# Gate matrix laid out by chunk of experts and read in three pieces; odd rows of v in u's buffers

## The chip, the cores and the metric

One core of a Trainium2 chip runs the whole program. The metric is the device time of one execution in microseconds (us); less is better.

## The reference

One layer of a streaming encoder over 512 tokens of width 1024: token mixing (sparse attention and pooling), then channel mixing by PEER: each token picks, in 8 heads, its best 16 of 128 x 128 = 16384 experts, each expert being one row of u and one of v. The part that matters here, cut down:

```python
def peer_ffn(h, w_q, sub_keys, u, v):
    ...
    expert = (i1 * N_KEYS + i2).reshape(TOKEN_BLOCK, PEER_HEADS * PEER_TOPK)
    gate = jax.nn.softmax(best_s, axis=-1).reshape(...)
    u_sel = u[expert]
    v_sel = v[expert]
    act = jax.nn.gelu(jnp.einsum('nd,ned->ne', hx, u_sel), approximate=False)
    return jnp.einsum('ne,ned->nd', gate * act, v_sel)
```

## The kernel before

For three of the four blocks of 128 tokens (384 tokens, `ND`) the kernel does not gather: it computes the activation of all 16384 experts for all tokens and multiplies it by a dense matrix of gates that is zero where a token did not pick an expert. The fourth block gathers its 128 rows of u and of v per token (the sparse branch, `sparse`, gathers issued by POOL, sums on DVE). The experts come in 128 groups of 128 (`NEXP`); c is the number of a group throughout.

Stages, in order of time (us from the start of the span):

- to about 480: token mixing, norms, the keys of PEER, the first dense activations.
- about 480 to 740, the gates stage: `gates` builds the dense gates, 16 tokens at a time, into a tile `st` of [128, 128 groups, 16 tokens], 8 KB a partition, and line 629 writes it to the DRAM tile `gd`: 24 writes of 1 MB. Beside it run the dense activations (`dense_acts`): the transposed u of a group is loaded (`ue`, 512 KB, line 527, two buffers in pool `up`), split by ACT into a high part (`uhe`, 517) and by DVE into the rest (`ule`, 518), and multiplied (`pse`, 554 to 556). 59 groups are done here; 22 of their results (`ad`) go to DRAM.
- about 740 to 1598, the contraction: for each c the gates of the group multiply its activations (`gated`, line 727), the product is split (`Wh`, 737, and `Wl`, 739), the row block v of the group (512 KB, line 735) is loaded and split by ACT (`vh`, 738) and DVE (`vl`, 740), and 18 matmuls (line 748, `contract`) add into six accumulators. For c from 0 to 21 the loop only reads an earlier activation back (`gelu..b`, 778); for c from 22 to 90 it also computes one of the remaining activations (538 to 540); from c = 91 on (the tail) it is contraction alone, beside the last of the sparse branch.

The gates come back from `gd` in 16 reads, one for 8 groups (`GJ`), line 725: 24 runs of 512 bytes a partition, 1.5 MB. Their tile `g` has two buffers in pool `vp`, and so has `v`.

The order on DVE, PE and ACT in the contraction is written out by hand (the `manual_schedule` block at the end). SP issues all plain loads and stores, in one queue, in an order that a scheduler derives; an issue that waits (for its buffer to be read out, say) holds everything behind it on SP. A load of v(c+2) waits until `vl(c)` has read its buffer; with two buffers, at most two v are on their way or in use.

```python
            gts[0] = vp.tile([P, ND // GT, GJ, GT], F32, tag="g", name=f"g{c}")
            nc.sync.dma_start(out=gts[0], in_=gd[:, :, c:c + GJ, :].rearrange("g p e t -> p g e t"))
```

Of the kernel before, what the change touches and what calls it, by code (L numbers as in the profile page):

```python
# [9 lines left out]
F32 = mybir.dt.float32  # L10
# [6 lines left out]
ALU = mybir.AluOpType  # L17
# [3 lines left out]
P = 128  # L21
S = 512
D = 1024
DT = D // P
# [9 lines left out]
DENSE = 3  # L34
ND = DENSE * P
NEXP = 128
GT = 16
GJ = 8
# [7 lines left out]
RATE = 3.0  # L46
REST = 7
UPS = 2
SCALED = 14
STB = 2  # L50
FILLS = [(2, 1), (2, 5), (3, 0), (3, 1), (3, 2), (3, 3), (3, 4), (3, 5), (3, 6), (3, 7)]
# [14 lines left out]
def layer(ctx, tc, xT, cvec, w_ada, cols, consts, w_in, w_grp, w_up, w_out, w_pq, subk, u, uT, v, out):  # L66
    nc = tc.nc
    V, A, T, G = nc.vector, nc.scalar, nc.tensor, nc.gpsimd
# [10 lines left out]
    g2row = tc.dram_tile([1, D], F32, name="g2row")  # L79
    x2d = tc.dram_tile([TB, P, D], F32, name="x2d")  # L80
    ad = tc.dram_tile([SPILL, P, ND], F32, name="ad")
    gd = tc.dram_tile([ND // GT, P, NEXP, GT], F32, name="gd")
    nc.sync.dma_start(out=col, in_=cols)
    eps = keep.tile([P, 1], F32, name="eps")
    V.memset(eps, EPS)
# [4 lines left out]
    with ExitStack() as pre:  # L90
# [83 lines left out]
        blocks += [(f"ga{j}", w_in[B_GA + j], DT) for j in range(2)]  # L174
        blocks += [(f"up{j}", w_up[1, j], 4) for j in range(UPS)]
        blocks += [(f"ga{j}", w_in[B_GA + j], DT) for j in range(2, DT)]
        blocks += [(f"up{j}", w_up[1, j], 4) for j in range(UPS, DT)]
        blocks += [(f"ua{j}", w_up[0, j], 4) for j in range(DT)]
# [22 lines left out]
        with ExitStack() as mix:  # L201
# [207 lines left out]
            def up_pool(j):  # L409
                V.tensor_tensor(yp[:, j, :], yp[:, j, :], linear(f"up{j}", pTh, pTl, 4), op=ALU.mult)  # L410

            for j in range(DT):
                tc.keep_in_program_order(A.activation(yp[:, j, :], yp[:, j, :], AF.Sigmoid))
                if j < UPS:
                    up_pool(j)
# [46 lines left out]

            fills = [partial(gate, j) for j in range(2, DT)] + [partial(up_pool, j) for j in range(UPS, DT)]
            for tb in range(TB):
# [47 lines left out]
    up = ctx.enter_context(tc.tile_pool(name="up", bufs=2, side="right", reuse_waits="tile"))  # L512
# [18 lines left out]
    def multiply(w, n, name):  # L531
        return multiplies([w], n, [name])[0]
# [11 lines left out]
    KEPT = HOLD - 1  # L544
# [23 lines left out]
    with ExitStack() as win:  # L568
# [23 lines left out]
        def gates(tb):  # L592

            tr = ptr.tile([P, 4, P], F32, tag="tr", name=f"gtr{tb}")
            for i, x in enumerate(sel[tb]):
                T.transpose(tr[:, i, :], x, ident)

            keys = oh.tile([P, 2, P], F16, tag="keys", name=f"keys{tb}", bufs=1)
            part = oh.tile([P, 2, P], F16, tag="part", name=f"part{tb}", bufs=1)
            gs = oh.tile([P, P], F32, tag="gs", name=f"gs{tb}", bufs=1)  # L600
            A.copy(keys, tr[:, 0:2, :])
            A.activation(gs, tr[:, 2, :], AF.Copy, scale=2.0 ** SCALED)
            A.copy(part[:, 0, :], gs)
            V.tensor_tensor(part[:, 1, :], gs, part[:, 0, :], op=ALU.subtract)

            full = [P, 4, NEXP, 2]
            pairs = lambda x, t: x[:, t:t + 8].rearrange("p (q j) -> p q j", j=2).unsqueeze(2).to_broadcast(full)
            numbers = irep.unsqueeze(1).to_broadcast(full)
            for g in range(P // GT):
                st = oh.tile([P, NEXP, GT], F32, tag="st", name=f"st{tb}_{g}", bufs=STB)  # L610
                for t8 in range(0, GT, 8):
                    t = g * GT + t8
                    one, two = [oh.tile(full, F16, tag=f"on{i}", name=f"on{i}_{tb}_{t}") for i in range(2)]
                    V.tensor_tensor(one, numbers, pairs(keys[:, 0, :], t), op=ALU.is_equal)  # L614
                    V.tensor_tensor(two, numbers, pairs(keys[:, 1, :], t), op=ALU.is_equal)  # L615
                    gated = []
                    for i in range(2):
                        x = oh.tile(full, F16, tag=f"oa{i}", name=f"oa{i}_{tb}_{t}")
                        gated.append(x)
                        V.tensor_tensor(x, one, pairs(part[:, i, :], t), op=ALU.mult)  # L620
                    for t4 in range(0, 8, 4):
                        ps = pgm.tile([P, 4, P], F32, tag="gm", name=f"gm{tb}_{t + t4}")
                        for k in range(4):
                            q, j = (t4 + k) // 2, k % 2
                            for i in range(2):
                                T.matmul(ps[:, k, :], two[:, q, :, j], gated[i][:, q, :, j], start=(i == 0), stop=(i == 1))  # L626
                        A.activation(st[:, :, t8 + t4:t8 + t4 + 4].rearrange("p e t -> p t e"), ps, AF.Copy, scale=2.0 ** -SCALED)  # L627
                        yield
                nc.sync.dma_start(out=gd[tb * (P // GT) + g], in_=st)

        sel = {}

# [45 lines left out]
    vp = ctx.enter_context(tc.tile_pool(name="vp", bufs=2, reuse_waits="tile"))  # L678
# [33 lines left out]
    def residual(tb):  # L712
        x = gp.tile([P, D], F32, tag="row", name=f"xr{tb}")
        nc.sync.dma_start(out=x, in_=x2d[tb])
        return x

    rows = sparse()
    gts = {}
    wei = {}

    def gated(c):

        if c % GJ == 0:
            gts[0] = vp.tile([P, ND // GT, GJ, GT], F32, tag="g", name=f"g{c}")
            nc.sync.dma_start(out=gts[0], in_=gd[:, :, c:c + GJ, :].rearrange("g p e t -> p g e t"))
        wv = gelus[c].rearrange("p (g t) -> p g t", t=GT)
        V.tensor_tensor(wv, wv, gts[0][:, :, c % GJ, :], op=ALU.mult)

    def weights(c):

        last = c == NEXP - 1
        vr = vp.tile([P, D], F32, tag="v", name=f"v{c}")
        vh, vl = [(gp if last else vp).tile([P, D], F32R, tag="row" if last else t, name=f"{t}{c}") for t in ("vh", "vl")]
        wh, wl = [(hold if last else vp).tile([P, ND], F32R, tag="gelu" if last else t, name=f"{t}{c}") for t in ("Wh", "Wl")]
        nc.sync.dma_start(out=vr, in_=v[c * P:(c + 1) * P, :])
        w = gelus.pop(c)
        A.activation(wh, w, AF.Copy)  # L737
        A.activation(vh, vr, AF.Copy)  # L738
        V.tensor_tensor(wl, w, wh.bitcast(F32), op=ALU.subtract)
        V.tensor_tensor(vl, vr, vh.bitcast(F32), op=ALU.subtract)  # L740
        wei[c] = (vh, vl, wh, wl)
# [11 lines left out]
    def ahead(c):  # L753
        if c < NEXP:
            pending[c] = fetch(uT[c], f"e{c}", tc.keep_in_program_order)

    with tc.manual_schedule(engines={mybir.EngineType.DVE, mybir.EngineType.PE, mybir.EngineType.Activation}):
        gated(0)
        weights(0)
        gated(1)  # L760
        V.tensor_copy(ei3, e3)
        due = -DELAY
        late = (2 * P + DELAY - EARLY * SPILL - RATE * (NEXP - KEPT - SPILL)) / (KEPT - REST)
        for c in range(NEXP):
            a = c + KEPT
            if c + 1 < NEXP:
                weights(c + 1)
            if c + 2 < NEXP:
                gated(c + 2)
            if c >= SPILL - 1:  # L770
                ahead(a + 1)
            due += EARLY if c < SPILL else RATE if c < NEXP - KEPT else late
            while due >= 1:
                next(rows, None)
                due -= 1
            if c < SPILL:
                gelus[a] = hold.tile([P, ND], F32, tag="gelu", name=f"gelu{a}b")
                nc.sync.dma_start(out=gelus[a], in_=ad[c])
            elif a < NEXP:
                gelus[a] = hold.tile([P, ND], F32, tag="gelu", name=f"gelu{a}")  # L780
                A.activation(gelus[a], multiply(pending.pop(a), ND, f"e{a}"), AF.Gelu)
            if c == NEXP - REST + 1:
                for _ in rows:
                    pass
                x = residual(DENSE)
                for i in range(2):
                    finish(DENSE, x, i, sacc[:, i * 512:(i + 1) * 512])
            if c < NEXP - 2:
                for tb in range(DENSE):
                    contract(c, tb)  # L790

        xs = [residual(tb) for tb in range(DENSE)]
        for tb in range(DENSE):
            for halves in (((0,), (1,)) if tb == DENSE - 1 else ((0, 1),)):
                for c in (NEXP - 2, NEXP - 1):
                    contract(c, tb, halves)
                for i in halves:
                    finish(tb, xs[tb], i, acc[tb][i])
# [172 lines left out]
```

## Time and profile before

| what | value |
|---|---|
| time, three runs | 1596.89, 1600.07, 1604.06 us (median 1600.07) |
| profiled execution: its time | 1600.14 us |
| profiled execution: its span, first to last instruction | 1598.3 us |
| PE busy | 1540.0 us, 96% of the span |
| DVE busy | 1311.6 us, 82% |
| ACT busy | 691.3 us, 43% |
| POOL busy | 326.1 us, 20% |
| DMA | 393.91 MB, mean 246 GB/s |
| mean granted TensorE clock | 0.991 |
| share of the chain that ended last: PE, DVE, DMA | 48%, 10%, 5% |

The profile lists how long each engine was busy, the chain of work that ended last (followed back from the last instruction to what released each step), the groups of instructions with their durations, and what each engine waited for. PE is the matrix engine, ACT and DVE work on vectors, POOL issues the gathers, SP (SPq) issues the other transfers. The 5% of DMA in the chain is loads of v.

### The profile page before, as it was taken

What the parts mean: (1) busy time and instruction counts of PE and PEld (TensorE: products, weight loads), DVE (VectorE), ACT (ScalarE), POOL (GpSimd) and SP (SyncE); (2) the same over time, 40 slices, a digit from 0 to 9 for tenths busy, and PEclk for the clock granted to TensorE, in tenths of its full rate; (3) what the DMA queues carried; (4) which work ended last, traced back from release to release, by engine and by line L of the source; (5) the groups of instructions that cost most, each with busy time, mean ns of one, the idle gap of its engine ahead of it and who ended that gap; (6) DMA issues with size and microseconds to landing.
All of it is one profiled execution on the core that took longest, in us unless ns stands there. A gap on an engine that the chain in (4) does not pass through costs nothing.

```text
span 1598.3 us, 22373 instructions
## 1 busy us (share of the span) xinstructions
PE 1540.0 (96%) x7977; PEld 1311.7 (82%) x7977; DVE 1311.6 (82%) x2658; ACT 691.3 (43%) x993; POOL 326.1 (20%) x318
## 2 busy tenths in 40 slices
PE   5999999999999999999999999999999999999998
PEld 3678766786789888899778999999999999987776
DVE  7799776658999999995668888888888888887777
ACT  4543445534446675674333333333333333333332
POOL 0000000000000000001113444444544445442320
PEclk9999999999999999999999999999999999999999
DMA  8412654333235454669889999999999999987874
GB/s 309 165 66 86 214 186 121 117 148 119 66 119 195 163 190 173 229 234 322 301 288 340 322 364 332 339 360 316 361 336 337 355 318 363 339 289 261 273 274 171
DMA packets 155105, 393.91 MB, mean 246 GB/s; under 512 B 13041, under 2 KB 67953, under 8 KB 151922
## 3 DMA queue, kind: packets, MB, share of 16 engines
q1 hardware_dynamic: 118130, 258.25, 46.5%
q0 software_dynamic: 36864, 134.23, 23.8%
q8 instruction: 62, 1.02, 0.3%
q14 instruction: 49, 0.40, 0.1%
HBM read 358.75 MB, written 33.69 MB: 246 GB/s over the span
## 4 chain that ended last, share of the span: by engine, by line
PE 48%; DVE 10%; DMA 5%; ACT 1%; issue 1%; SPq 0%; ACTq 0%; DVEq 0%
PE acc L748 28%; PE pse L540 6%; PE pse L539 6%; PE pse L538 6%; DMA v<-v 5%; DVE oa L620 2%; DVE ule L518 2%; DVE on L614 1%; DVE on L615 1%; ACT vh L738 1%; DVE vl L740 1%; PE pse L556 1%; PE pse L555 1%; PE pse L554 1%; PE gm L626 0%
## 5 line engine op out<-in xcount | busy, mean ns | idle before, releaser
L689 POOL DMA_INDIRECT ur<-u,ei x128 | 158.0, 1234 | 638.7 <-ACT Wh L737 395.0
L748 PE MATMUL acc<-vh,Wh 128*128 128x512 f32 x768 | 240.3, 394 | 14.6 <-ACT vh L738 14.6
L748 PE MATMUL acc<-vl,Wh 128*128 128x512 f32 x768 | 241.2, 395 | 2.0 <-DVE vl L740 1.9
L748 PE MATMUL acc<-vh,Wl 128*128 128x512 f32 x768 | 240.1, 394 | 0.0
L740 DVE TENSOR_TENSOR vl<-v,vh 128x1024 fp32r<-128x1024 f32 x128 | 156.9, 1226 | 83.0 <-ACT vh L738 70.7
L697 POOL DMA_INDIRECT vr<-v,ei x128 | 165.2, 1291 | 232.7 <-DVE sacc L702 204.2
L540 PE MATMUL pse<-h2h,ule 128*128 128x384 f32 x552 | 185.1, 335 | 0.0
L539 PE MATMUL pse<-h2l,uhe 128*128 128x384 f32 x552 | 184.6, 334 | 0.0
L538 PE MATMUL pse<-h2h,uhe 128*128 128x384 f32 x552 | 184.4, 334 | 0.0
L737 ACT ACTIVATE Wh<-gelu 128x384 fp32r<-128x384 f32 x106 | 55.6, 525 | 290.1 <-PE acc L748 187.5
L748 PEld LDWEIGHTS acc<-vh,Wh 128*128 128x128 f32 x768 | 144.7, 190 | 41.6 <-ACT vh L738 16.7
L748 PEld LDWEIGHTS acc<-vl,Wh 128*128 128x128 f32 x768 | 145.7, 191 | 35.3 <-DVE vl L740 5.3
L748 PEld LDWEIGHTS acc<-vh,Wl 128*128 128x128 f32 x768 | 146.2, 190 | 30.9
L518 DVE TENSOR_TENSOR ule<-ue,uhe 128x1024 fp32r<-128x1024 f32 x128 | 155.9, 1218 | 19.0 <-ACT uhe L517 19.0
L554 PE MATMUL pse<-h2h,uhe 128*128 128x384 f32 x472 | 166.2, 352 | 1.0 <-ACT gelu L563 1.0
L556 PE MATMUL pse<-h2h,ule 128*128 128x384 f32 x472 | 161.1, 342 | 4.7 <-DVE ule L518 4.5
L702 DVE SCALAR_TENSOR_TENSOR sacc<-vr,wt,sacc 128x1024 f32<-128x1024 f32 x127 | 162.8, 1282 | 2.4
L555 PE MATMUL pse<-h2l,uhe 128*128 128x384 f32 x472 | 159.6, 338 | 0.0
L517 ACT ACTIVATE uhe<-ue 128x1024 fp32r<-128x1024 f32 x128 | 134.8, 1053 | 53.8 <-PE pse L555 36.0
L691 DVE SCALAR_TENSOR_TENSOR ur<-ur,hx 128x1024 f32<-128x1024 f32 x128 | 150.7, 1220 | 1.5 <-DMA ur<-u,ei 1.5
L738 ACT ACTIVATE vh<-v 128x1024 fp32r<-128x1024 f32 x128 | 135.7, 1060 | 36.0 <-DMA v<-v 35.7
L627 ACT ACTIVATE st<-gm 128x512 f32<-128x512 f32 x96 | 101.2, 1092 | 53.9 <-PE gm L626 49.6
(412 smaller groups left out, 2757.3 us busy)
## 6 DMA issues: line engine op xcount, KB each, us to landing
ue<-uT SPq DMA_DIRECT2D x128, 512.0 KB
v<-v SPq DMA_DIRECT2D x128, 512.0 KB
wada<-w_ada SPq DMA_DIRECT2D x48, 512.0 KB
gd<-st SPq DMA_DIRECT2D x24, 1024.0 KB
g<-gd SPq DMA_DIRECT2D x16, 1536.0 KB
ad<-gelu SPq DMA_DIRECT2D x22, 192.0 KB
wgp<-w_in SPq DMA_DIRECT2D x8, 512.0 KB
wga<-w_in SPq DMA_DIRECT2D x8, 512.0 KB
```

What stands on the lines that cost most here:

```text
L518: V.tensor_tensor(lo, src, hi.bitcast(F32), op=ALU.subtract)
L538: T.matmul(p, hi[:, k, :], h2h[:, k, :n], start=(k == 0), stop=False)
L539: T.matmul(p, hi[:, k, :], h2l[:, k, :n], start=False, stop=False)
L540: T.matmul(p, lo[:, k, :], h2h[:, k, :n], start=False, stop=(k == DT - 1))
L554: T.matmul(ps, hi[:, k, :], h2h[:, k, :ND], start=(k == 0), stop=False)
L555: T.matmul(ps, hi[:, k, :], h2l[:, k, :ND], start=False, stop=False)
L556: T.matmul(ps, lo[:, k, :], h2h[:, k, :ND], start=False, stop=(k == DT - 1))
L689: G.indirect_dma_start(out=ur, out_offset=None, in_=u, in_offset=bass.IndirectOffsetOnAxis(ap=ei3[:, k:k + 1], axis=0))
L697: G.indirect_dma_start(out=vr, out_offset=None, in_=v, in_offset=bass.IndirectOffsetOnAxis(ap=ei3[:, k:k + 1], axis=0))
L702: V.scalar_tensor_tensor(sacc, vr, wt[:, k:k + 1], sacc, op0=ALU.mult, op1=ALU.add)
L740: V.tensor_tensor(vl, vr, vh.bitcast(F32), op=ALU.subtract)
L748: T.matmul(acc[tb][i], x[:, t], y[:, i * 512:(i + 1) * 512], start=(c == 0 and n == 0), stop=(c == NEXP - 1 and n == 2))
```

## The change

1. `gd` gets another shape: [16 chunks of 8 groups, 128 partitions, 24 blocks of 16 tokens, 8, 16]. The whole of a chunk is now 12 KB in one run for a partition. A write of `st` (line 629) becomes 16 runs of 512 bytes a partition instead of one of 8 KB.
2. The read of a chunk's gates becomes three reads (`gate_piece`), each 4 KB in one run a partition, 512 KB. They are asked for in the groups 1, 3 and 5 of the chunk before; chunk 0's before the contraction starts. The tile, its size and its two buffers stay.
3. From c = 93 on, odd c load v into the two `u` buffers of pool `up`, which the last u has left; even c keep the two buffers of `vp`. So the tail has four buffers for v.

```diff
-    gd = tc.dram_tile([ND // GT, P, NEXP, GT], F32, name="gd")
+    gd = tc.dram_tile([NEXP // GJ, P, ND // GT, GJ, GT], F32, name="gd")
...
-                nc.sync.dma_start(out=gd[tb * (P // GT) + g], in_=st)
+                nc.sync.dma_start(out=gd[:, :, tb * (P // GT) + g].rearrange("c p e t -> p c (e t)"),
+                                  in_=st.rearrange("p (c e) t -> p c (e t)", e=GJ))
...
+    GP = P // GT
+
+    def gate_piece(n, i):
+
+        if i == 0:
+            gts[n] = vp.tile([P, ND // GT, GJ, GT], F32, tag="g", name=f"g{n}")
+        nc.sync.dma_start(out=gts[n][:, i * GP:(i + 1) * GP], in_=gd[n, :, i * GP:(i + 1) * GP])
 
     def gated(c):
 
-        if c % GJ == 0:
-            gts[0] = vp.tile([P, ND // GT, GJ, GT], F32, tag="g", name=f"g{c}")
-            nc.sync.dma_start(out=gts[0], in_=gd[:, :, c:c + GJ, :].rearrange("g p e t -> p g e t"))
+        n, e = c // GJ, c % GJ
+        if e in (1, 3, 5) and n + 1 < NEXP // GJ:
+            gate_piece(n + 1, e // 2)
         wv = gelus[c].rearrange("p (g t) -> p g t", t=GT)
-        V.tensor_tensor(wv, wv, gts[0][:, :, c % GJ, :], op=ALU.mult)
+        V.tensor_tensor(wv, wv, gts[n][:, :, e, :], op=ALU.mult)
...
-        vr = vp.tile([P, D], F32, tag="v", name=f"v{c}")
+        if c >= NEXP - KEPT + UGAP and c % 2:
+            vr = up.tile([P, DT, P], F32, tag="u", name=f"v{c}").rearrange("p k e -> p (k e)")
+        else:
+            vr = vp.tile([P, D], F32, tag="v", name=f"v{c}")
...
+        for i in range(DENSE):
+            gate_piece(0, i)
         gated(0)
```

The instructions of PE and DVE, and their order, stay as they were (two splits of u change places on ACT). What moves is SP's queue. In the tail, around the gates of groups 104 to 111 (`g104` before, `g13`, the chunk's number, after), SP has before:

```order
L735 DMA v94_13412<-v 128x1024
L735 DMA v95_13444<-v 128x1024
L735 DMA v96_13481<-v 128x1024
L725 DMA g104_13715<-gd_71 128x24x128
L735 DMA v97_13513<-v 128x1024
L735 DMA v98_13545<-v 128x1024
L735 DMA v99_13577<-v 128x1024
```

and after the change:

```order
L747 DMA v95_13472<-v 128x1024
L747 DMA v94_13440<-v 128x1024
L747 DMA v96_13507<-v 128x1024
L747 DMA v97_13541<-v 128x1024
L747 DMA v98_13573<-v 128x1024
L728 DMA g13_13517<-gd_71 128x1024 x2
L747 DMA v99_13606<-v 128x1024
L728 DMA g13_13517<-gd_71 128x1024
L747 DMA v100_13638<-v 128x1024
```

Two pieces stand together behind v98, the third behind v99; v95, which now has another buffer, stands ahead of v94. In the first part of the contraction, around the gates of groups 16 to 23, SP has before:

```order
L778 DMA gelu44b_7940<-ad_70 128x384
L735 DMA v8_7926<-v 128x1024
L725 DMA g16_8171<-gd_71 128x24x128
L735 DMA v9_7960<-v 128x1024
L778 DMA gelu45b_7974<-ad_70 128x384
```

and after:

```order
L792 DMA gelu44b_7946<-ad_70 128x384
L747 DMA v8_7930<-v 128x1024
L728 DMA g2_7940<-gd_71 128x1024
L792 DMA gelu45b_7980<-ad_70 128x384
L728 DMA g2_7940<-gd_71 128x1024
L747 DMA v9_7966<-v 128x1024
L792 DMA gelu46b_8015<-ad_70 128x384
L728 DMA g2_7940<-gd_71 128x1024
L747 DMA v10_8000<-v 128x1024
```

Here v9 stands behind two pieces and one read of an activation, v10 behind the third piece.

## Rows read from the trace of the kernel before

**Rows 1.** Page part 5, costliest groups: the two splits of v
```profile
L740 DVE TENSOR_TENSOR vl<-v,vh 128x1024 fp32r<-128x1024 f32 x128 | 156.9, 1226 | 83.0 <-ACT vh L738 70.7
L738 ACT ACTIVATE vh<-v 128x1024 fp32r<-128x1024 f32 x128 | 135.7, 1060 | 36.0 <-DMA v<-v 35.7
```

**Rows 2.** Chain in order of time, contraction: start us, us, what
```profile
772.64 5.54 DMA v<-v
...
780.62 10.44 DMA v<-v
...
816.21 11.28 DMA v<-v
...
1410.72 4.09 PE acc L748 x18
...
1437.73 12.29 DMA v<-v
...
1477.46 11.53 DMA v<-v
...
1515.75 11.76 DMA v<-v
...
1529.98 56.94 PE acc L748 x243
```

**Rows 3.** Timeline of SP: start us, us, engine, line, operation, count
```profile
776.72 0.37 SPq L725 DMA_DIRECT2D g<-gd  x1
780.62 3.04 SPq L735 DMA_DIRECT2D v<-v  x1
...
1434.12 0.38 SPq L725 DMA_DIRECT2D g<-gd  x1
```

**Rows 4.** Timeline of ACT, line 737, first and last of each stretch read
```profile
785.69 0.53 ACT L737 ACTIVATE Wh<-gelu 128x384 fp32r<-128x384 f32 x1 [2.28 <-PE acc L748]
...
801.16 0.53 ACT L737 ACTIVATE Wh<-gelu 128x384 fp32r<-128x384 f32 x1 [2.31 <-PE acc L748]
...
821.56 0.53 ACT L737 ACTIVATE Wh<-gelu 128x384 fp32r<-128x384 f32 x1 [1.89 <-PE acc L748]
...
836.38 0.53 ACT L737 ACTIVATE Wh<-gelu 128x384 fp32r<-128x384 f32 x1 [4.42 <-PE acc L748]
...
1439.01 0.53 ACT L737 ACTIVATE Wh<-gelu 128x384 fp32r<-128x384 f32 x1 [2.56 <-PE acc L748]
...
1458.32 0.53 ACT L737 ACTIVATE Wh<-gelu 128x384 fp32r<-128x384 f32 x1 [3.83 <-PE acc L748]
...
1478.74 0.53 ACT L737 ACTIVATE Wh<-gelu 128x384 fp32r<-128x384 f32 x1 [2.56 <-PE acc L748]
...
1496.63 0.53 ACT L737 ACTIVATE Wh<-gelu 128x384 fp32r<-128x384 f32 x1 [3.16 <-PE acc L748]
...
1517.03 0.53 ACT L737 ACTIVATE Wh<-gelu 128x384 fp32r<-128x384 f32 x1 [2.56 <-PE acc L748]
...
1551.32 0.53 ACT L737 ACTIVATE Wh<-gelu 128x384 fp32r<-128x384 f32 x1 [2.32 <-PE acc L748]
```

**Rows 5.** Windows: stretch, length, PE, PEld, DVE, ACT, POOL busy (count), PEclk, DMA share, GB/s
```profile
560.00:600.00 40.00, 38.33 (x297) 34.86 (x296) 40.00 (x119) 28.97 (x35) 0.00 (x0) 1.00 0.54 193
...
920.00:1400.00 480.00, 480.00 (x2443) 438.87 (x2442) 405.69 (x497) 173.91 (x235) 224.49 (x174) 1.00 0.97 343
...
1445.00:1450.00 5.00, 2.54 (x12) 1.76 (x10) 0.00 (x0) 0.00 (x0) 0.24 (x1) 1.00 1.01 403
```

**Rows 6.** DMA queue view, 812.6 to 819 us: packets, MB, share of 16 engines
```profile
q1 hardware_dynamic: 1520, 1.30, 72.4%
```

**Rows 7.** The same view, 1555 to 1565 us
```profile
q1 hardware_dynamic: 451, 1.62, 50.8%
```

**Rows 8.** Timeline of SP, gates stage
```profile
494.68 0.33 SPq L629 DMA_DIRECT2D gd<-st  x1
495.10 4.94 SPq L527 DMA_DIRECT2D ue<-uT  x2
```

**Rows 9.** DMA view, 494.5 to 504 us: busy tenths in 40 slices
```profile
DMA  0000996999599796956999940092799982000000
```

**Rows 10.** Timeline of ACT, gates stage: the split of that u
```profile
503.48 1.06 ACT L517 ACTIVATE uhe<-ue 128x1024 fp32r<-128x1024 f32 x1
```

More of the change, by code (lines that the diff above doesn't have):

```diff
@@ L48 @@
 UPS = 2
+UGAP = 2
 SCALED = 14
```

## The prediction

> **What bounds the kernel now.** I read the chain first, then the timelines of SP and ACT, then the DMA views. In the contraction PE sets the pace: the 18 matmuls of a group take 4.09 us, and from 920 to 1400 us PE is busy for all of the 480 us [rows 2, 5]. The chain leaves PE where it goes through a load of v. Five of those loads take 10.44 to 12.29 us, against 5.54 us for one with no gates ahead of it [rows 2]. SP shows why: the read of a chunk's gates is issued at 776.72 and at 1434.12, and the next v, at 780.62 and 1437.73, is the one that takes 10.44 and 12.29 us [rows 2, 3]. The first of these also holds SP for 3.04 us where other issues take some 0.3 [rows 3].
>
> How late may a v be? It is issued when its buffer is free, that is when the rest split of v two groups earlier ends; it must land, be split by ACT (1.06) and by DVE (1.23) within two groups. 2 x 4.09 - 1.06 - 1.23 - 0.1 for gaps = 5.8 us [rows 1, 2]. A clean load (5.54) just fits; one behind the gates is 4.6 to 6.5 us late.
>
> What that costs PE I read from ACT's split of the weights, which follows PE group by group [rows 4]. From 785.69 to 801.16 lie 3 groups: 15.47 - 3 x 4.09 = 3.20 us lost. From 821.56 to 836.38 lie 2: 6.64. In the tail, 3 groups from 1439.01: 7.04; 3 from 1478.74: 5.62; 7 from 1517.03: 5.66. The start of the contraction loses 9.84 us, the tail 18.32, together **28.16 us**. Between groups 22 and 90, where a group takes twice as long because u is multiplied too, nothing is lost.
>
> **The change part by part.** The sum is made against the profiled execution's 1600.14 us (1.84 us more than its span), which is the median of the runs, 1600.07, to within 0.1.
>
> *Reads of 4 KB.* The reads are 16 x 1.5 MB before and 48 x 512 KB after, the same bytes. In a stretch with much of the gates' read, SP's queue kept 72.4% of 16 engines busy for 6.4 us with 1520 packets and 1.30 MB; taken as packets of 4 KB and 512 bytes, that is about 146 and 1374 [rows 6]. In a stretch with v alone 1.62 MB, or 396 packets of 4 KB, took 50.8% of 16 x 10 us, 0.205 us each [rows 7]. So the first stretch spent 74.1 - 146 x 0.205 = 44.1 us on 1374 small packets, 0.032 us each: 4 KB in small pieces cost 0.257 us against 0.205. The reads get 20% cheaper for the engines. This alone takes 20% of the 6.75 us (12.29 - 5.54) by which the worst v was delayed, 1.4 us.
> The Trainium skill (DMA: Bandwidth & Descriptors, Specifications) gives 512 bytes as the transfer size from which the line rate is reached. By it this part would bring nothing, each piece below would delay v 25% longer (1.8 us where I take 1.4, 2.25 where I take 1.8), and the sum would end some 2.5 us higher, at 1580; the rows put 512 bytes 25% above 4 KB, so I take the rows.
>
> *Three pieces, start of the contraction.* v9 and v10 now stand behind pieces of a third (the second pair of orders above). A whole read delayed v by 10.44 - 5.54 = 4.9 and 11.28 - 5.54 = 5.7 us [rows 2], mean 5.3; a third at 80% is 1.4. So v9 takes about 6.9 us, 1.2 more than the 5.8 that are free. I count that as PE's loss once in each of the two chunks, 2.4 us. From below it is 0, if the rest split may be that much later than the first matmul; from above twice that, 4.8, since v8 and v10 share a buffer and two delays may add. The value is taken in the middle, as it is nearest to the single delay of the rows. **Gain 9.84 - 2.4 = 7.4 us.**
>
> *Tail: pieces and four buffers.* The queue goes in pairs, v98 with v99, v100 with v101. An even v still has 5.8 us. An odd v has been free for long but stands behind its even neighbour on SP, so it gets one group more, 9.9 us. v99 has two pieces and v98 ahead: 5.54 + 6.75 x 2/3 x 0.8 + 1.3 (v98's 0.52 MB at the 403 GB/s of 1445 to 1450 [rows 5]) = 10.4, late by 0.5. v100 has one piece ahead: 5.54 + 1.8 = 7.3, late by 1.5. One delay of 1 us per chunk is my value, 3 us for three chunks; the ends are 0 and 2.1 x 3 = 6.3. **Gain 18.32 - 3 = 15.3 us.**
>
> *The writes.* The same 24 MB, in 2048 packets of 512 bytes where there were 128 of 8 KB. No row shows such a write. As a bound from the read's price, 2048 / 16 x 0.032 = 4.1 us a write. Today a write is issued at 494.68 with a u right behind it at 495.10; by slice 24 (500.2 us) both are in, so 1.57 MB took some 4.8 us and the write 3.2 of it [rows 8, 9]. The u is used at 503.48 [rows 10]: 3.3 us to spare, 2.4 with the slower write. I take 0. It cannot be a gain, as no step waits for a write there; if the cover went, DVE would pay in full, since it is busy for 40.00 of 40 us in that stage [rows 5].
>
> *Edits at nothing.* Groups 22 to 90: twice the matmul time per group covers the loads, and PE has no idle time to give back [rows 5]. The gates were already asked for a chunk ahead, so reading ahead is not new. The last two v move ahead of two stores of the result: from 1529.98 on the chain is PE alone for 56.94 us [rows 2], so nothing follows. 32 more issues on SP at about 0.3 us lie in a queue that mostly waits for buffers.
>
> Sum: 1600.14 - 7.4 - 15.3 = 1577.4; I forecast **1577 us**. Its own bounds are 1600.14 - 28.16 = 1572 with no loss left, and 1572 + 4.8 + 6.3 = 1583 with both upper ends.
>
> **The rivals.**
> *A, half stays.* The pieces are not spread: two stand together and the third follows one v later, so within two groups the queue still carries 1.5 MB of gates. If SP's order, not the number of buffers, decides, each stop shrinks to half: 1600.14 - 14.1 = 1586 us. For it speaks the order itself; against it that v98 has passed before the first piece. Chance 0.2.
>
> *B, the bytes decide.* In the tail 8 groups need 4.2 MB of v, 1.6 of gates and at least 4.2 of gathered rows in 32.7 us, some 305 GB/s; pieces don't change that. If the engines are as good as full, the stops only move to another v, and what is left is the 20% of cheaper packets: 0.2 x 28 = 5.6 us, 1594 us, no measurable change. Against it: 343 GB/s over 480 us and 403 over 5 [rows 5].
> The Trainium skill (DMA: Bandwidth & Descriptors, Bandwidth) has the rule that transfers should be batched to 1 MiB or more to reach 75% of the peak, which speaks for B, as pieces of 512 KB would use the engines worse than one of 1.5 MB. Most of the traffic from 920 to 1400 us is loads of 512 KB, and the share is 0.97 at 343 GB/s, so the trace does not bear it out where transfers overlap. Chance 0.09.
>
> *C, the writes come late: slower.* If a small packet costs twice as much written as read, 0.064 us, a write takes 8.2 us, 5.0 more than today, and the u behind it comes 5.0 - 3.3 = 1.7 us late. DVE has no room there, so 24 times that is 41 us: 1577 + 41 = 1618 us. It begins to cost at (3.2 + 3.3) x 16 / 2048 = 0.051 us a packet. For it: the DVE row, and that not every u has so much to spare. Against it: DMA's share there is only 0.54 [rows 5], and most u are not right behind a write. Chance 0.06.
>
> **How the numbers follow.** The forecast gets what remains, 0.65. A difference under 0.5%, 8 us, can't be told from none; the bounds are 1592 and 1608. The forecast's case lies under 1592 wholly, of A's 0.2 about 0.17; B is "same" with the rest of A; C is slower. So faster 0.82, same 0.12, slower 0.06. The range 1570 to 1590 holds the forecast's case and most of A.
>
> **What would show it.** Right: on ACT's line 737 no gap far over 4.09 us from 1420 on, and one or two of about 1 us between 785 and 840; no load of v over 8 us in the chain unless it is an odd one in the tail; the gates stage as long as before, with the first matmul of the contraction at the same time. Wrong: a chain that still has v loads of 10 us (A or B, told apart by whether they stand behind pieces), or waits for u and DVE idle time between 480 and 740 us (C).

## The result, and the profile after

Four runs of the changed kernel took 1574.20 to 1575.62 us, median **1574.58**; four of the kernel before, beside them, had a median of 1598.94. The ratio is **0.9844**, 95% interval [0.9819, 0.9869]: faster by 1.3 to 1.8%. The forecast was 1577, range 1570 to 1590. The profiled execution took 1574.86 us with a span of 1573.1, against 1600.14 and 1598.3; the sums below are of spans.

The page of the changed kernel: part 4 (shares of the chain), then part 5, the splits of v (they answer to [rows 1]), then part 6, issues with their count, size and median us to landing.

```profile
PE 51%; DVE 10%; DMA 2%; ACT 1%; issue 0%; SPq 0%; ACTq 0%; DVEq 0%
...
L752 DVE TENSOR_TENSOR vl<-v,vh 128x1024 fp32r<-128x1024 f32 x128 | 156.8, 1225 | 59.0 <-ACT vh L750 58.8
...
L750 ACT ACTIVATE vh<-v 128x1024 fp32r<-128x1024 f32 x128 | 135.9, 1062 | 9.8 <-DMA v<-v 9.4
...
v<-v SPq DMA_DIRECT2D x128, 512.0 KB, 5.8
...
gd<-st SPq DMA_DIRECT2D x24, 1024.0 KB, 5.9
g<-gd SPq DMA_DIRECT2D x48, 512.0 KB, 8.0
```

DMA's share of the chain fell from 5% to 2%, and the time for which ACT stood waiting for v from 35.7 us to 9.4. The splits themselves cost what they did.

Its chain in order of time (start us, us, what), to be read against [rows 2]:

```profile
735.10 7.17 DMA g<-gd
...
777.22 5.92 DMA v<-v
...
785.58 8.14 DMA v<-v
...
814.81 8.29 DMA v<-v
...
1412.20 149.47 PE acc L760 x659
```

No load of v is left in the tail: from 1412 us PE runs 659 matmuls with no gap, where the kernel before left PE three times. At the start two loads of 8.1 and 8.3 us stand where 10.44 and 11.28 stood. The first row is new: a read of gates is now in the chain.

How much PE lost is read from ACT's split of the weights, as in [rows 4], but over whole stretches, so that one yardstick serves every kernel here: from group 2 to 22 (the start), and from 91 to 127 (the tail). The shortest stretches seen in any run are 81.65 and 150.26 us; what a kernel has above them is its loss. From group 22 to 91 every run takes 565.7 to 566.1. The four splits of the kernel before (start us, us, ..., idle before them):

```profile
757.08 0.53 ACT L737 ACTIVATE Wh<-gelu 128x384 fp32r<-128x384 f32 x1 [2.22 <-PE acc L748]
...
848.67 0.53 ACT L737 ACTIVATE Wh<-gelu 128x384 fp32r<-128x384 f32 x1 [2.56 <-PE acc L748]
...
1414.43 0.52 ACT L737 ACTIVATE Wh<-gelu 128x384 fp32r<-128x384 f32 x1 [3.19 <-DVE sacc L702]
...
1583.15 0.52 ACT L737 ACTIVATE Wh<-gelu 128x384 fp32r<-128x384 f32 x1 [1.76 <-DVE gelu L727]
```

and of the changed kernel, with two splits of v between them:

```profile
758.05 0.53 ACT L749 ACTIVATE Wh<-gelu 128x384 fp32r<-128x384 f32 x1 [3.09 <-PE acc L760]
...
788.58 1.06 ACT L750 ACTIVATE vh<-v 128x1024 fp32r<-128x1024 f32 x1 [1.40 <-DMA v<-v]
...
793.82 1.06 ACT L750 ACTIVATE vh<-v 128x1024 fp32r<-128x1024 f32 x1 [1.82 <-DMA v<-v]
...
841.89 0.53 ACT L749 ACTIVATE Wh<-gelu 128x384 fp32r<-128x384 f32 x1 [1.84 <-PE acc L760]
...
1407.65 0.52 ACT L749 ACTIVATE Wh<-gelu 128x384 fp32r<-128x384 f32 x1 [3.19 <-DVE sacc L704]
...
1557.91 0.53 ACT L749 ACTIVATE Wh<-gelu 128x384 fp32r<-128x384 f32 x1 [1.76 <-DVE gelu L736]
```

Start: 848.67 - 757.08 = 91.59, a loss of 9.94; now 83.84, a loss of 2.19. Tail: 168.72, a loss of 18.46; now 150.26, none. That is 26.2 us gained. The contraction begins 0.97 us later (758.05 against 757.08), and 26.2 - 1.0 = 25.2 is the difference of the spans, 1598.3 - 1573.1. So all of it is accounted for.

Windows of the changed kernel (columns as in [rows 5]):

```profile
480.00:720.00 240.00, 231.87 (x1777) 211.17 (x1776) 237.19 (x687) 161.54 (x200) 0.00 (x0) 1.00 0.64 198
920.00:1400.00 480.00, 480.00 (x2443) 438.79 (x2442) 405.37 (x494) 172.62 (x235) 221.07 (x174) 1.00 0.94 343
```

and the first of them before:

```profile
480.00:720.00 240.00, 231.76 (x1780) 210.95 (x1779) 237.19 (x688) 161.53 (x200) 0.00 (x0) 1.00 0.56 198
```

The writes in runs of 512 bytes show as DMA share: 0.64 against 0.56 at the same 198 GB/s. Over 240 us and 24 writes that is 0.08 x 240 / 24 = 0.8 us of all 16 engines per write. DVE is busy for the same 237.19 us: it costs nothing there. From 920 to 1400 the share fell from 0.97 to 0.94 for the same bytes.

### The profile page after: what moved, and what is told of

Same layout as the page of the kernel before. It is cut to its first block, busy times and chain, and to the rows that moved or that the text cites. A ratio compares the mean times of both kernels' runs of the same rounds, so it can differ in the third digit from the quotient of the medians.

```text
span 1573.1 us, 22413 instructions
## 1 busy us (share of the span) xinstructions
PE 1530.7 (97%) x7977; PEld 1307.4 (83%) x7977; DVE 1311.7 (83%) x2658; ACT 690.2 (44%) x993; POOL 324.9 (21%) x318
## 4 chain that ended last, share of the span: by engine, by line
PE 51%; DVE 10%; DMA 2%; ACT 1%; issue 0%; SPq 0%; ACTq 0%; DVEq 0%
PE acc L760 30%; PE pse L541 6%; PE pse L540 6%; PE pse L539 6%; DVE ule L519 2%; DVE oa L621 2%; DMA v<-v 1%; DVE on L615 1%; DVE on L616 1%; PE pse L557 1%; PE pse L556 1%; PE pse L555 1%; DMA g<-gd 0%; PE gm L627 0%; ACT vh L750 0%
## 5 line engine op out<-in xcount | busy, mean ns | idle before, releaser
L760 PE MATMUL acc<-vl,Wh 128*128 128x512 f32 x768 | 237.1, 390 | 1.0 <-DVE vl L752 1.0
L760 PE MATMUL acc<-vh,Wh 128*128 128x512 f32 x768 | 236.8, 389 | 0.0
L760 PEld LDWEIGHTS acc<-vl,Wh 128*128 128x128 f32 x768 | 143.9, 188 | 31.9 <-DVE vl L752 2.1
```

The source lines that it names most:

```text
L760: T.matmul(acc[tb][i], x[:, t], y[:, i * 512:(i + 1) * 512], start=(c == 0 and n == 0), stop=(c == NEXP - 1 and n == 2))
```

## Experiments

The change has three parts: the layout, the pieces, the tail's buffers. Kernels e1 to e4 and e7 switch these parts on and off, e5 and e6 ask what makes the gates' read slow, and e8 to e10 lend v the buffers at the start too. In the contraction the order of the instructions on PE and DVE is the same in all of them. Medians are in us, ratios are to the kernel before, run beside each; the losses are those of one profiled execution each, read as above, so where they vary from one execution to the next the median can lie apart from them.

| kernel | median | ratio, 95% | start | tail |
|---|---|---|---|---|
| before | 1598.94 to 1603.04 | | 9.94 | 18.46 |
| changed | 1574.58 | 0.9844 [0.9819, 0.9869] | 2.19 | 0 |
| pieces alone (e1) | 1587.85 | 0.9919 [0.9892, 0.9946] | 6.72 | 10.02 |
| layout alone (e2) | 1578.18 | 0.9868 [0.9842, 0.9894] | 0.93 | 3.59 |
| layout, pieces (e3) | 1576.77 | 0.9861 [0.9830, 0.9892] | 1.01 | 1.22 |
| tail's buffers alone (e4) | 1580.51 | 0.9880 [0.9855, 0.9906] | 8.58 | 0 |
| one read, runs of 4 KB (e5) | 1580.21 | 0.9855 [0.9823, 0.9887] | 4.25 | 6.57 |
| before, no gathers of v (e6) | 1581.58 | 0.9868 [0.9839, 0.9897] | 11.86 | 0 |
| layout, tail's buffers (e7) | 1575.34 | 0.9825 [0.9795, 0.9854] | 5.88 | 0 |
| layout, buffers at both ends (e8) | 1571.55 | 0.9807 [0.9783, 0.9831] | 0 | 0 |
| buffers at both ends alone (e9) | 1571.46 | 0.9805 [0.9778, 0.9832] | 0 | 0 |
| changed, buffers at both ends (e10) | 1572.03 | 0.9810 [0.9783, 0.9838] | 0 | 0 |
| changed, again (e11) | 1575.13 | 0.9832 [0.9804, 0.9860] | 4.97 | 0 |
| changed, writes twice (e12) | 1614.19 | 1.0081 [1.0052, 1.0109] | 5.51 | 0 |

(A fourth run of e5 took 2942.69 us, at a granted clock of 0.932 where its others have 0.996 and 0.997; it is not in the median.)

**e1, the pieces alone**, on the kernel before, with its layout:

```diff
+        if e in (1, 3, 5) and n + 1 < NEXP // GJ:
+            gate_piece(n + 1, e // 2)
```

> The kernel before with the read of a chunk's gates cut into three reads of 512 KB, issued as in the changed kernel; the old layout (runs of 512 bytes) and two buffers for v throughout. Theory (a v is late by the bytes of gates right ahead of it, a small packet costs 25% more): v9 and v17 are 1.8 us late instead of 4.6 to 5.5, so the start of the contraction loses 3 to 5 us instead of 9.84; in the tail v97 still has two pieces ahead and v98 one, 4.2 and 2.0 us late, so the tail loses 11 to 13 us instead of 18.3. About 1587 us. Rival 1 (cutting alone is the cure): under 4 us lost in the tail, 1578. Rival 2 (cutting does nothing, the bytes decide): 1598.

The time came as the theory has it, 1587.85, from a start worse and a tail better than it said. Pieces alone take away 3.2 of 9.9 us and 8.4 of 18.5, and the chain still goes through loads of 9.5 to 10.9 us in the tail:

```profile
1439.91 9.69 DMA v<-v
...
1470.72 9.53 DMA v<-v
...
1505.57 10.92 DMA v<-v
```

**e2, the layout alone**: the changed kernel with one whole read at the head of each chunk, asked for when it was before, and two buffers for v.

```diff
-        if e in (1, 3, 5) and n + 1 < NEXP // GJ:
-            gate_piece(n + 1, e // 2)
+        if e == 0:
+            gts[n] = vp.tile([P, ND // GT, GJ, GT], F32, tag="g", name=f"g{n}")
+            nc.sync.dma_start(out=gts[n], in_=gd[n])
```

> The kernel before with the new layout alone: one read of 1.5 MB per chunk, now 12 KB in one run a partition, and the writes in runs of 512 bytes; two buffers for v throughout. Theory (20% fewer engine-us per read): each stop shrinks by 1.1 to 1.4 us, 5 stops, so the start loses about 7.5 us and the tail 14 to 15; 1593 us. Rival 1 (512 bytes are as good as long runs): nothing, 1599. Rival 2 (many small packets are the cause): most of the 28 us gone, 1577.

The theory's 1593 fell and Rival 2's 1577 held: the same 1.5 MB in the same place in the queue, in runs of 12 KB for 512 bytes, removes 14.9 of the tail's 18.5 us. (The profiled execution is the fastest of e2's four, 1574.02 us; the others took 1577.06 to 1579.59, and where they lost the difference is not known.) What differs while the read runs is in the DMA queue view (packets, MB, share of 16 engines; q1 is SP's queue, q0 the gathers'). A share is the sum of the packets' times, so it can pass 100% where packets overlap. The kernel before, 1438 to 1440 us and 1442 to 1444:

```profile
q1 hardware_dynamic: 1016, 0.56, 98.0%
...
q1 hardware_dynamic: 651, 0.33, 58.7%
q0 software_dynamic: 109, 0.39, 52.0%
```

e2, 1459 to 1461 us, 1461 to 1462 and 1462 to 1463:

```profile
q1 hardware_dynamic: 61, 0.63, 89.0%
...
q1 hardware_dynamic: 32, 0.39, 93.4%
...
q1 hardware_dynamic: 24, 0.27, 64.9%
q0 software_dynamic: 27, 0.11, 27.7%
```

In both kernels the first us of the read meet no gathers: there is no row of q0 from 1438 to 1440 before, nor from 1459 to 1462 in e2. By itself the read moves 0.28 MB a us in small packets (0.56 in 2 us) and 0.39 in long runs (from 1461 to 1462; in the two us before, some packets are still v's). Beside gathers it moves 0.17 MB a us in small packets (0.33 in 2 us), at 59% against the gathers' 52%, and 0.27 in long runs, at 65% against 28%. That is one us only, as most of the long read is in before the gathers come. In windows of 1 us the last packets of the read lie at about 1447 us before, 13 us after its issue at 1434.12 [rows 3], and at about 1464.5 in e2, 9 us after its issue at 1455.51. The v behind it takes 8.74 us in e2's chain (the load at 1459.12), where it took 12.29.

**e3, layout and pieces**, without the tail's buffers:

```diff
-        if c >= NEXP - KEPT + UGAP and c % 2:
+        if False:
```

> The changed kernel without u's buffers for v: new layout, three pieces, two buffers for v in the tail too. Theory (buffers are needed in the tail, as two pieces stand together there): the start loses 2.1 us as in the changed kernel; in the tail v97 has two pieces ahead, 3.3 us late, so the tail loses 8 to 10 us; 1583 us. Rival (pieces and layout do all, the buffers nothing): the tail loses under 1 us, 1575.

The tail lost 1.2 us, not 8 to 10. With runs of 4 KB two pieces that stand together stop nothing much, and against e2 the pieces bring nothing that the times can tell (0.9861 and 0.9868).

**e4, the tail's buffers alone**, on the kernel before:

```diff
+        if c >= NEXP - KEPT + UGAP and c % 2:
+            vr = up.tile([P, DT, P], F32, tag="u", name=f"v{c}").rearrange("p k e -> p (k e)")
```

> The kernel before with u's buffers for odd v in the tail alone: old layout, one read of 1.5 MB. Theory (depth is the cure in the tail): the start loses 9.84 us as before; in the tail v99 needs about 13.6 us and has 9.9 and what PE's own two buffers of split v give, so the tail loses 3 to 8 us instead of 18.3; 1587 us. Rival 1 (buffers alone cure the tail): under 1 us, 1581. Rival 2 (SP's order decides, an odd v waits behind an even one): 15 or more, 1597.

The theory's 3 to 8 fell, Rival 1 held: the old layout, the whole read and all its small packets stay, and the tail loses nothing. The chain's last part is the same row as in the changed kernel:

```profile
1417.97 149.47 PE acc L760 x659
```

**e5, runs of 4 KB**: one read as in e2, two buffers, but three runs of 4 KB a partition.

```diff
-    gd = tc.dram_tile([NEXP // GJ, P, ND // GT, GJ, GT], F32, name="gd")
+    gd = tc.dram_tile([NEXP // GJ, DENSE, P, P // GT, GJ, GT], F32, name="gd")
```

> As the run with the layout alone, but the chunk's gates lie in three blocks, so that its one read of 1.5 MB has three runs of 4 KB a partition and not one of 12 KB; two buffers for v. New theory (the queues of the plain loads and of the gathers take turns, packet by packet or about so, so that gathers that are on their way pass a read of small packets for its whole length; before, gathers took half of the engines while the gates' read ran, and 14% to 50% with 12 KB runs): 4 KB lies between, the tail loses 6 to 12 us (18.5 with 512 bytes, 3.6 with 12 KB). Rival (only the engine time of a packet matters, and 4 KB has no more of it than 12 KB): the same as with 12 KB, 3 to 4 us in the tail and about 1 in the start.

A tail of 6.57 lies in the theory's range, between 512 bytes (18.46) and 12 KB (3.59). Its rival is not ruled out, though: the times do not tell 4 KB from 12 KB (0.9855 and 0.9868), and each of the two losses is of one execution, e2's of its fastest. The queues from 1467 to 1469 us, without gathers, and from 1469 to 1471:

```profile
q1 hardware_dynamic: 168, 0.69, 98.2%
...
q1 hardware_dynamic: 120, 0.48, 59.8%
q0 software_dynamic: 76, 0.31, 39.3%
```

By itself SP's queue moves 0.34 MB a us, between 512 bytes (0.28) and 12 KB (0.39). Beside gathers it moves 0.48 MB in 2 us, where it moved 0.33 with 512 bytes. Its share is no larger (60% and 59%), so the bytes follow the theory of shares and the share does not. (The packets of v have 4 KB too, and the row does not tell them from the read's.)

**e6, the kernel before without the gathers of v** in the sparse branch:

```diff
-            vr = gp.tile([P, D], F32, tag="row", name=f"vr{k}")
-            G.indirect_dma_start(out=vr, out_offset=None, in_=v, ...)
+            if k == 0:
+                vr = gp.tile([P, D], F32, tag="row", name=f"vr{k}")
+                G.indirect_dma_start(out=vr, out_offset=None, in_=v, ...)
```

> The kernel before (old layout, one read, two buffers), with the gathers of v's rows for the sparse branch left out: row 0 is gathered once and used 128 times, so the sparse branch's sum is another one; DVE's work is the same. New theory (half of what a read of the gates costs is gathers that share the engines with it): with none in the tail, the gates' read takes 6 us instead of 10, the v behind it 8 instead of 12, and the tail loses 0 to 5 us instead of 18.5; the start, whose gathers of u are still there, loses 9 to 10 as before. Rival (the small packets themselves are slow, gathers or not): the tail loses 14 or more.

The tail loses nothing with the small packets, the whole read and two buffers all in place; the last packets of the same read lie at about 1442.5, 8 us after its issue at 1434.57. In the same view, 1438.5 to 1440.5 us:

```profile
q1 hardware_dynamic: 1129, 0.58, 112.2%
```

So in the tail small packets cost only where gathers run beside them. The start, whose gathers are those of u and stay, lost 11.9. One thing this run does not separate: without the gathers of v the engines also have fewer bytes to move.

**e7, layout and tail's buffers, no pieces**: the edit of e2 alone, on the changed kernel.

> The changed kernel without the three pieces: new layout, one read of 12 KB runs, u's buffers for odd v in the tail. Both theories: the start loses 0.9 us as with the layout alone (2.1 in the changed kernel), the tail 0 as in the changed kernel, and the contraction starts 0.6 to 1 us earlier after the last write of the gates, since no third piece of chunk 0 stands behind a load of u: 1572.5 us, 2 below the changed kernel. Rival (the pieces help in some place not seen): 1575 or more.

1575.34, not 1572.5: the tail is clean, but the start lost 5.9 us where e2, with the same queue at the start, lost 0.9. The four runs of e7 fall in two pairs (1572.79 and 1573.00, 1577.68 and 1578.08), and the profiled one is of the slower. With two buffers the start's loss changes from one execution to the next; its loads of v in the chain took 8.59 and 10.93 us here, 8.40 alone in e2.

**e8, the buffers at both ends**, with the layout and without pieces: odd groups 1 to 19 use u's buffers too (the loop computes no new activation there, so u needs none).

```diff
-        if c >= NEXP - KEPT + UGAP and c % 2:
+        if c % 2 and (c < SPILL - UGAP or c >= NEXP - KEPT + UGAP):
```

> As the run before this one, and odd v take u's buffers in the start of the contraction too (c from 1 to 19), between the last u of the gates stage and the first of the loop. Theory (depth hides every stop): the start loses under 0.3 us, the tail 0; 1571.5 us. Rival (odd v now stand behind even ones on SP, and the first u of the loop waits for v19's buffer): the start loses 1 us or more, or a stop appears where u comes back, at c = 21 to 24.

Nothing is lost at either end, 1571.55.

**e9, the buffers at both ends alone**: that condition on the kernel before, with its layout and its whole read. Nothing else is changed.

> The kernel before (old layout, one read of 1.5 MB in runs of 512 bytes) with u's buffers for odd v in the start of the contraction (c from 1 to 19) and in the tail. Theory (depth hides a stop of any of the sizes seen, whatever the layout): the start loses under 0.5 us, the tail 0; as fast as the run with the new layout and both buffers, 1571.5 us. Rival (the start needs shorter reads too, since its gathers of u and the reads of earlier activations stand in the same queues): the start loses 2 to 5 us, 1575.

1571.46, the same as e8: where every v has slack, neither layout nor pieces are needed. Its chain:

```profile
750.75 89.77 PE acc L760 x396
...
1406.37 149.47 PE acc L760 x659
```

396 matmuls are the first 22 groups without a gap. This beats both kernels: its runs (1569.03 to 1571.79) lie under all those of e11 (1574.28 to 1577.96), on the same chip; the difference of 3.7 us is 0.23%, and the intervals of the two ratios overlap.

**e10, the changed kernel with the buffers at both ends**:

> The changed kernel with u's buffers for odd v in the start of the contraction too (c from 1 to 19): depth, layout and pieces. Theory: the start loses under 0.3 us, the tail 0; what is left against the run without pieces is the third piece of chunk 0 behind a load of u, 0.6 to 1 us: 1572 us. Rival (the pieces cost nothing): no difference to depth alone.

1572.03, not to be told from e9: on top of the buffers, layout and pieces bring nothing.

**e11, the changed kernel again**, beside e9 and e10:

> The changed kernel once more, as the yardstick of this call: 1574.5 us, start loses 2.1 us and tail 0. If the theory of the start is right, it is 2 to 3 us above the two runs with deeper buffers in the start; if the start's 2.1 us vary from run to run as those with the layout and one read did (0.9 and 5.8), it is from 1 to 5 above.

The start lost 4.97 us in this execution, 2.19 in the first. Its loads of v in the chain include

```profile
784.15 7.00 DMA v<-v
...
812.72 9.87 DMA v<-v
```

against 8.14 and 8.29: which load is late, and by how much, varies. Why is open.

**e12, every write of gates issued twice**, the second to a DRAM tile that nobody reads:

```diff
+                nc.sync.dma_start(out=gd2[:, :, tb * (P // GT) + g].rearrange("c p e t -> p c (e t)"),
+                                  in_=st.rearrange("p (c e) t -> p c (e t)", e=GJ))
```

> The changed kernel with every write of the gates issued a second time, into another tensor, in the same runs of 512 bytes: 24 MB more between 480 and 740 us. Theory of the prediction (a u right behind a write has some 2.4 us to spare, a second write takes 3.2 to 4.1): the u behind comes 1 to 2 us late and DVE has no room, so the gates stage gets 10 to 30 us longer: 1585 to 1605. Rival (most u are asked for early enough, or DVE's order leaves room): under 5 us, 1575 to 1580.

1614.19, over the theory's upper end: the last write is issued at 764.27 us instead of 726.16, 38 us later. The edit did more than add writes: the scheduler put the gates stage in another order too, and from 505 us on DVE and ACT, later also PE, do part of their work in another order than in the changed kernel. Waits of e12 from 480 to 780 us (who for whom: us in all, times, longest):

```profile
DVE ule L520 <- ACT uhe L519: 38.4, 22, 10.1
ACT uhe L519 <- DMA ue<-uT: 31.7, 19, 3.7
...
ACT st L629 <- DMA gd<-st: 2.5, 2, 1.3
```

and of the changed kernel from 480 to 745:

```profile
DVE ule L519 <- ACT uhe L518: 10.4, 9, 4.1
ACT uhe L518 <- DMA ue<-uT: 3.0, 1, 3.0
```

u comes late, DVE waits, and DVE has no time to give: the chain of Rival C, set off by twice the write. The tile `st`, which both writes read, is not what is waited for (2.5 us in all). SP's timeline there shows that the second issue also holds the queue (us in the second column), with u behind it:

```profile
503.78 0.38 SPq L631 DMA_DIRECT2D gd<-st  x1
504.21 5.65 SPq L633 DMA_DIRECT2D gd<-st  x1
510.15 4.02 SPq L529 DMA_DIRECT2D ue<-uT  x2
```

So the room beside one write seems small, as a second one goes with 38 / 24 = 1.6 us each. Bytes, packets and SP's hold all grew and the order changed; which of them did it was not tried.

## Why the prediction was right, and where it was not

**What bounds.** Right. v behind the gates was what PE waited for; 28.4 us by the longer yardstick, 28.16 forecast, and e8, e9 and e10 gain all of it. Their 1571.5 to 1572.0 is the floor that the prediction worked out as 1572.

**Reads of 4 KB.** This step failed: the term was far too small. The price per packet was right: from 1438 to 1440 us 1016 packets took 98% of 16 x 2 us, 0.031 us each, 0.032 forecast. But I let the 20% of engine time stand for the delay of v (1.4 of 6.75 us). Of the tail's 18.5 us, runs of 4 KB alone, as the change reads them, took 11.9 (e5), and runs of 12 KB 14.9 (e2), where one fifth was forecast. What I left out is the gathers: without them the small packets cost the tail nothing (e6). Beside them the read's last packet came 13 us after its issue, with 12 KB runs 9. Two things lie in this that the runs do not separate. A read in long runs is faster by itself (0.34 MB a us with 4 KB and 0.39 with 12 KB, against 0.28), so that less of it is left when the gathers come, and beside them it goes on faster too (0.24 and 0.27 against 0.17). The stretch of [rows 6] already had the gathers in it, in the same view:

```profile
q0 software_dynamic: 145, 0.53, 24.6%
```

I took the price of a packet from that stretch and did not ask who had the rest of the engines.
The Trainium skill (DMA: Bandwidth & Descriptors, Specifications) gives 512 bytes as enough for the line rate. This case does not bear that out: by itself the read moved 0.28 MB a us in packets of 512 bytes, 0.39 in packets of 12 KB, and beside gathers it fell further behind.
The Trainium skill (DMA: Bandwidth & Descriptors, Queues, rings and completion order) says that each engine takes turns between the queues it has work for, one whole packet at a time. Packets of 12 KB, with 65% beside the gathers' 28%, go the way of that rule. The profile's packets of 512 bytes do not take turns one by one with the gathers' rows of 4 KB: 651 went by beside 109 from 1442 to 1444 us.

**Three pieces, start.** Gain forecast 7.4, measured 7.75 in one execution and 4.97 in the other: right in size, with a residue (2.4 forecast, 4.8 at most) that varies from 2.2 to 5.0. v9 was reckoned at 6.9 us: it was issued at 781.30, and its split waited for it until 788.58. Which part did it is not shown: the layout alone left 0.93 in e2 and 5.88 with the same start in e7, the pieces alone 6.72 in e1, in one execution each.

**Tail.** Gain forecast 15.3, measured 18.46; the residue of 3 us is 0. The time that a v has was too small here: I left an even v its 5.8 us and gave an odd one 9.9. But since the odd ones have buffers of their own, an even v waits for the rest split of v four groups earlier, as an odd one does. In the changed kernel v98 is issued 0.03 us after the rest split of v94 ends, and split by ACT long after (the timelines of SP and ACT):

```profile
1426.88 0.33 SPq L747 DMA_DIRECT2D v<-v  x1
...
1440.85 1.06 ACT L750 ACTIVATE vh<-v 128x1024 fp32r<-128x1024 f32 x1
```

So it has 14.0 us (5.8 and two more groups of 4.09), and v99, issued at 1430.95 and split at 1444.93, the same. The 10.4 and 7.3 us that I reckoned for the loads fit into that, and so do the 13.6 that e4's expectation gave to v99 in the old layout. e4 shows that the buffers alone give all of the gain.

**Gates ahead.** Not foreseen: +1.0 us before the contraction. I said that its first matmul would come at the same time. The third piece of chunk 0 stands on SP behind a load of u (the timeline of SP in the changed kernel):

```profile
734.72 0.33 SPq L528 DMA_DIRECT2D ue<-uT  x1
735.10 0.49 SPq L728 DMA_DIRECT2D g<-gd  x1
```

It is issued at 735.10, where the whole read was at 732.89, and it is in the chain. From the issue of the last write of gates to group 2's split it is 30.8 to 31.2 us in eight profiles with a whole read, 31.4 to 31.9 in five with pieces (the changed kernel has 31.9 and, as e11, 31.4). The errors of the three terms, -3.2 (tail), -0.3 (start) and +1.0, make 1577.4 into 1574.9, the profiled 1574.86.

**The writes** at nothing: right, with 0.8 us of the engines for each where 0.9 was reckoned. e12 suggests that little room was left.

**Rivals.** A (half stays, 1586) fell for the change, but it is what the pieces alone give: 1587.85, with 16.7 of 28.4 us left. SP's order decides while the reads are slow and v has no slack. B (the bytes decide) fell: e9 moves the same bytes and loses nothing, and with 343 GB/s either way the share went down. C fell for one write; with two, u came late and DVE waited as it says, in a kernel whose order had changed too.

**Signs.** No load of v over 8 us was to be in the chain: two were, 8.14 and 8.29, both at the start. And the contraction's first matmul came later (Gates ahead, above), and the gaps of about 1 us between 785 and 840 were three (0.8, 1.2 and 1.9). The rest came as said.

So the total was right for a reason partly wrong: three parts, each of which shortens the same wait, were added up as if the buffers and the pieces did most. They replace one another. That the sum came within 2.5 us is partly luck: parts that replace one another can be mis-sized without a trace in their sum, and the tail's error and the late first matmul have opposite signs. Alone, layout, buffers and pieces take from the tail 14.9, 18.5 and 8.4 us of the same 18.5. Pieces with buffers but in the old layout were not tried.

## What to carry to other kernels

Where a load lands a little later than its buffers allow, give it slack first: e9, one condition that lends it idle buffers, was worth as much as all else together. Where two queues compete, ask what length of packet each has: here a read in short runs was slower by itself and slower still beside the other queue's long ones, and what stood behind it in its queue paid. Price parts that shorten the same wait as alternatives, not as a sum, and test each alone.

## What was not expected of the hardware

- From issue to last packet the same 1.5 MB took some 13 us in runs of 512 bytes beside gathers (the kernel before), 8 without gathers (e6), and 9 in runs of 12 KB beside gathers (e2).
- Cutting a read of 1.5 MB into three of 512 KB made nothing slower that could be seen but the start of the contraction (0.5 to 1.0 us), and the loads of v among the pieces came sooner: the tail's loss went from 18.5 to 10.0 us (e1 against before).
- One and the same kernel lost 2.2 us at the start in one execution and 5.0 in another, where a wait was near its limit. Where it had slack (e8 to e10, one execution each) nothing was lost.
- A second write of 2048 packets right behind the first held SP's issue for 1.75 to 5.65 us (e12, the seven from 480 to 560 us), where a first one takes 0.4 to 0.7.
